# Four edits to the order of work in a tuned encoder layer: a PSUM copy moved to ScalarE, accumulating stores held back, a mixture put ahead, more places for split weights

## The chip, the cores and the metric

One core of a Trainium2 chip runs the whole kernel. The metric is the device time of one execution in microseconds (us), as the median of the runs shown. All matrix work is done in float32 accuracy by splitting each operand into a high and a low part, so one product is three matmuls: high by high, high by low, low by high.

## The reference, cut to what matters

The reference is one encoder layer with two branches side by side, applied to a prompt batch of 1024 rows and a sample batch of 512 rows with the same weights:

```python
h = rms_norm(x, pre_w)
cols = einsum('bsd,dc->bsc', h, w_in)              # one wide input projection
m_qk, m_v, m_o, m_z, m_i, m_f, a_qkv, a_z, gate = split(cols, ...)
y_m = mlstm_mixer(silu(conv(m_qk)), m_v, ...) * silu(m_z)      # branch A, both directions
y_a = dilated_attention(a_qkv, rel_table) * silu(a_z)          # branch B, three dilations
p_m = y_m @ w_pm
p_a = y_a @ w_pa
merged = sigmoid(gate_a) * p_m + sigmoid(gate_b) * p_a
y = x + rms_norm(merged @ w_out, post_w)
# the mixture inside dilated_attention, for 3 groups g:
w = exp(mx - max_g mx);  y_a = sum_g(w * o) / sum_g(w * den)
```

The outputs are y_prompt (1024 x 1024) and y_sample (512 x 1024).

## The kernel before, in words

The prompt batch is "the long set", the sample batch "the short set". The program runs in stages.

**First stage, up to some 965 us.** The input projection of the long set is done by the Strassen-Winograd scheme, two column units of 128 at a time, in `unit_pair` (from L827; 38 pairs). A pair is seven products m1, m6, m2, m7, m5, m4, m3 of 12 matmuls (128x512) each. The products lie in PSUM banks, the tile `d`. m2 is accumulated onto m1's bank and m3 onto m5's, so m3's first matmul can start only when m5 has been read out of that bank. `u2` and `u3` (in the profile the tile `pu`) are running sums in SBUF, `c` holds the four result blocks, `q[i][j]` are views of `c`. The weights come as `pw_raw` and `psum_w` and are split into high and low parts `phla` and `phlb` by ScalarE (L766 and L795 for the high part) and VectorE (L767 and L796 for the low part). After every pair the columns get what their kind asks for: convolution and tanh (`conv_unit`, L880 to L884), SiLU and others.

At the end of this stage the short set's input is turned (`turn_in`, L351 on TensorE, L357 on ScalarE, L358 on VectorE: the tiles `H`), and its own weights from `w_in` begin to be loaded into the two staging buffers `wraw` (L288) and split: the high part `wh` by ScalarE (L299), the low part `wl` (L305) by VectorE or, here, GpSimd.

**Middle.** The two branches of both sets, up to some 2028 us.

**Last stage, 2028 us to the end.** The short set's projections with `w_pm` (`proj_m`), `w_pa` (`proj_a`) and `w_out` (`final`) run on TensorE. Beside them stands what is left of other work:

- the 16 accumulating stores of y_prompt (L2494, 256 KB each; closures in the list `self.adds`, filled when the long set's output rows are done at L2493). A store adds to DRAM and is issued by GpSimd. `proj_m` pops one of them at every fourth step.
- GpSimd's queue, which also issues the loads of the pre-split weights (`wl<-pre`, `wh<-pre`, L832), of `w_pm` (`wraw<-w_pm`, L288), and of the mixture's inputs (`og_b` into V0a and V1a, `az_b`, `gt_b` into `gab`, all L276).
- the mixture of the short set, `combine`, four rounds of 128 rows. A round is `weigh` (a chain of small operations on `cw` and `wd`, L2086 to L2096), three `mix` (L2103), two `add` (L2109), then `turn` (L2114: four transposes `tp` on TensorE; L2116 on VectorE multiplies the result by `az`). Its result goes to DRAM (`ym_b`) by a store on SyncE's queue, and is loaded again from there as rows `ymr` and `sraw` (L276) to be split by ScalarE (L2209) and VectorE (L2210) for `proj_a`. I call the four turns turn 0 to turn 3; the last one is split straight from SBUF (L2120), without its 128 columns going through DRAM.

The order of each engine's instructions is fixed when the program is built: a scheduler places them by its own estimate of times and by priority. `high_priority()` lets an instruction go ahead of others that are ready, and `issue_after(x)` keeps an instruction behind x in its engine's order; it is no wait on the chip by itself. An engine runs its instructions in that order, so one that waits holds up those behind it.

Of the kernel before, what the change touches and what calls it, by code (L numbers as in the profile page):

```python
# [24 lines left out]
AF = mybir.ActivationFunctionType  # L25
# [181 lines left out]
class Net:  # L207
# [627 lines left out]
    def unit_pair(self, weights, H, sb, cp, ps):  # L835

        nc = self.nc
        wa, wb, (a11, a12), (s1, s2), s, places, (u2, u3) = weights
        split = self.pair_split

        def product(m, w, onto=None):
            p = onto or ps.tile([P, BLK], F32, name="d")
            for k in range(4):
                self.mm3(p, (w[0][:, k], w[1][:, k]), (H[0][m][:, k], H[1][m][:, k]), onto is None and k == 0, k == 3,
                         skip_group_check=onto is not None)
            return p

        nc.gpsimd.tensor_sub(s[:, 1], wa[:, 1], s[:, 1])
        s3, a22 = split(wb, places[0])
        c = [cp.tile([P, 2 + 2 * BLK], F32, name="c") for _ in range(2)]  # L850
        q = [[c[j][:, 1 + b * BLK:1 + (b + 1) * BLK] for b in range(2)] for j in range(2)]
        m1 = product(B11, a11)
        with self.tc.high_priority():
            nc.scalar.activation(u2, m1, AF.Copy)  # L854
        m6 = product(T2, s2)
        nc.vector.tensor_add(u2, u2, m6)
        m2 = product(B21, a12, m1)
        nc.scalar.activation(q[0][0], m2, AF.Copy)
        m7 = product(T3, s3)
        with self.tc.high_priority():  # L860
            nc.vector.tensor_sub(u3, u2, m7)
        m5 = product(T1, s1)
        with self.tc.high_priority():
            nc.vector.tensor_add(q[1][1], u3, m5)  # L864
        m4 = product(T4, a22)
        nc.vector.tensor_add(q[1][0], u3, m4)
        s4, = split(s[:, 1:2], places[1])
        m3 = product(B22, s4, m5)
        nc.vector.tensor_add(q[0][1], u2, m3)
        return c  # L870
# [1195 lines left out]
    def combine(self, T, bank, cs, ys, sb, azs, slow):  # L2066
# [3 lines left out]
        nc = self.nc  # L2070
# [76 lines left out]
        for t in range(T.n):  # L2147
# [7 lines left out]
            for i, step in enumerate(steps):  # L2155
                with ExitStack() as st:
                    if i < 6:
                        for x in (*self.splits, self.sum, *self.state, *self.keyed) if slow else (self.evicted, summed):
                            if x is not None:
                                st.enter_context(self.tc.issue_after(x.ins))  # L2160
                    last = step()
                    if i == 5:
                        summed = last
                if i == 6 and t == T.n - 1 and T in self.direct:
                    self.mixed.add(T)
                if slow:
                    yield
                elif i == 5:
                    for g in range(2) if t else ():
                        ahead(t + 1, g)  # L2170
                    yield
                    if t:
                        ahead(t + 1, 2)
                    yield
                elif i == 6:
                    ahead(t)
                    yield
# [382 lines left out]
    def branches(self, T, b, odd, before):  # L2560
# [3 lines left out]
        nc, a = self.nc, self.a  # L2564
# [8 lines left out]
        def proj_m(weights):  # L2573
# [3 lines left out]
            for ct in range(KT):  # L2577
                wm = weights()
                pm = self.dense()
                for k in range(KT):  # L2580
                    if k % 4 == 3 and self.adds:
                        self.adds.pop(0)()
                    c = slice(k * P, (k + 1) * P)
                    hi, lo = yb[k // 4]
                    self.mm3(pm, (wm[0][:, c], wm[1][:, c]), (hi[:, k % 4], lo[:, k % 4]), k == 0, k == KT - 1)
# [7 lines left out]
        def proj_a(weights):  # L2593
            for ct in range(KT):
                if ct % 2 == 0:
                    wa = weights()
                pa = self.dense()
                mh, ml = yb[ct // 4]
                yh, yl = ya[0]
# [447 lines left out]
```

## Time and profile before

| what | value |
|---|---|
| runs | 2189.52 us median of 3 (2189.27 to 2189.61) |
| profiled execution, its own time | 2190.96 us |
| profiled execution, span from the first to the last instruction | 2189.2 us, mean granted TensorE clock 0.997 |
| TensorE busy | 2161.0 us of the span (99%), 11530 matmuls |
| VectorE, ScalarE, GpSimd busy | 1503.4, 1106.3, 801.0 us (69%, 51%, 37%) |
| DMA | 469 MB, 214 GB/s on average |

The profiled execution is 1.44 us above the median of the runs. Its span leaves 1.8 us for what lies around the first and last instruction. The page gives for each group of instructions its busy time, the mean of one in ns and the idle time of its engine just before it with what ended it. A view of waits adds that idle time up by pairs of waiting and releasing lines; a timeline gives single rows: start, duration, engine, line, operation, tile, and in brackets the idle time before it with its releaser.

### The profile page before, as it was taken

The numbers are of one execution on the slowest core, as the hardware profiler recorded it, in microseconds if no ns is written. First come the engines' busy times: TensorE is split into PE (matmuls) and PEld (weight loads), VectorE is DVE, ScalarE is ACT, GpSimd is POOL, SyncE is SP. The second block draws the span as 40 slices with busy tenths as digits, with TensorE's granted clock in tenths as the row PEclk, the third lists the DMA queues.
The fourth block names the chain that finished last, engine by engine and source line by source line (L and its number), as shares of the span: only waits on it lengthen the run. The fifth ranks groups of instructions, "written<-read, shape, count | busy, mean of one in ns | idle before, by whom it ended". The sixth has DMA issues, their size and how long they took to land.

```text
span 2189.2 us, 33795 instructions
## 1 busy us (share of the span) xinstructions
PE 2161.0 (99%) x11530; PEld 1840.0 (84%) x11530; DVE 1503.4 (69%) x2923; ACT 1106.3 (51%) x2286; POOL 801.0 (37%) x1050
## 2 busy tenths in 40 slices
PE   9999999999999999999999999999999999999898
PEld 8988888888888888888888889999788888888686
DVE  8766575757788877537888766574667856675773
ACT  7322344454444444446777666665755544435422
POOL 1000444332333765325676660001035532331531
PEclk9999999999999999999999999999999999999999
DMA  5641687965456554358556558886767779886973
GB/s 215 191 141 65 210 271 245 301 218 182 177 190 217 198 188 175 135 192 270 176 184 228 164 159 263 254 244 179 224 237 239 266 254 330 287 275 208 265 239 114
DMA packets 234134, 469.04 MB, mean 214 GB/s; under 512 B 38281, under 2 KB 120393, under 8 KB 233834
## 3 DMA queue, kind: packets, MB, share of 16 engines
q1 hardware_dynamic: 199736, 343.81, 48.2%
q0 software_dynamic: 30624, 110.48, 15.7%
q10 hardware_dynamic: 3602, 12.59, 1.4%
q8 instruction: 91, 1.49, 0.3%
q14 instruction: 81, 0.66, 0.1%
HBM read 314.56 MB, written 156.43 MB: 215 GB/s over the span
## 4 chain that ended last, share of the span: by engine, by line
PE 90%; issue 3%; ACT 2%; DVE 2%; POOL 1%; DMA 1%; DVEq 0%; POOLq 0%; ACTq 0%
PE d L235 14%; PE d L237 13%; PE d L236 13%; PE dense L235 11%; PE dense L236 11%; PE dense L237 11%; PE lg L1851 2%; PE pt L1881 2%; PE o L1924 1%; PE num L235 1%; PE num L1544 1%; PE num L236 1%; PE num L237 1%; DMA wraw<-w_pm 1%; PE o L1903 1%
## 5 line engine op out<-in xcount | busy, mean ns | idle before, releaser
L235 PE MATMUL dense<-H,wh 128*128 128x512 f32 x712 | 288.6, 405 | 0.0
L237 PE MATMUL dense<-H,wl 128*128 128x512 f32 x712 | 279.0, 392 | 0.0
L236 PE MATMUL dense<-H,wh 128*128 128x512 f32 x664 | 260.4, 392 | 0.0
L235 PE MATMUL d<-Hh,phla 128*128 128x512 f32 x608 | 237.4, 390 | 0.4 <-ACT pu L854 0.3
L237 PE MATMUL d<-Hh,phla 128*128 128x512 f32 x608 | 236.6, 389 | 0.0
L236 PE MATMUL d<-Hl,phla 128*128 128x512 f32 x608 | 236.6, 389 | 0.0
L235 PE MATMUL d<-Hh,phlb 128*128 128x512 f32 x456 | 178.0, 390 | 3.6 <-DVE c L864 3.5
L237 PE MATMUL d<-Hh,phlb 128*128 128x512 f32 x456 | 177.5, 389 | 0.0
L236 PE MATMUL d<-Hl,phlb 128*128 128x512 f32 x456 | 177.4, 389 | 0.0
L237 PEld LDWEIGHTS dense<-H,wl 128*128 128x128 f32 x712 | 133.7, 188 | 29.9
L235 PEld LDWEIGHTS dense<-H,wh 128*128 128x128 f32 x712 | 134.3, 189 | 17.8 <-issue 0.9
L305 DVE TENSOR_TENSOR wl<-wraw,wh 128x1024 fp32r<-128x1024 f32 (+1 forms) x99 | 123.8, 1252 | 32.6 <-ACT wh L299 32.6
L785 POOL TENSOR_TENSOR psum_w<-pw_raw 128x512 f32<-128x512 f32 x38 | 52.4, 1380 | 245.0 <-DMA pw_raw<-w_in 144.1
L1870 DVE CUSTOM_DVE_ANT_0 ls<-lg,bias 128x256 f32<-128x256 f32 (+2 forms) x240 | 78.6, 350 | 90.8 <-PE lg L1851 67.3
L236 PEld LDWEIGHTS dense<-H,wh 128*128 128x128 f32 x664 | 125.3, 189 | 14.8 <-DVE H L2292 0.3
L235 PEld LDWEIGHTS d<-Hh,phla 128*128 128x128 f32 x608 | 114.1, 188 | 26.9 <-ACT pu L854 3.4
L237 PEld LDWEIGHTS d<-Hh,phla 128*128 128x128 f32 x608 | 114.1, 188 | 23.8
L236 PEld LDWEIGHTS d<-Hl,phla 128*128 128x128 f32 x608 | 114.2, 188 | 23.4
L299 ACT ACTIVATE wh<-wraw 128x1024 fp32r<-128x1024 f32 (+1 forms) x102 | 104.9, 1031 | 54.4 <-PE dense L236 39.1
L1874 ACT ACTIVATE ls<-ls,nm 128x256 f32<-128x256 f32 (+1 forms) x192 | 87.4, 456 | 76.2 <-DVE nm L1872 58.0
L235 PE MATMUL d<-v,Hh 128*128 128x484 f32 (+1 forms) x336 | 121.3, 361 | 0.1
L237 PE MATMUL d<-v,Hl 128*128 128x484 f32 (+1 forms) x336 | 120.6, 359 | 0.4 <-DVE Hl L475 0.4
(734 smaller groups left out, 5891.6 us busy)
## 6 DMA issues: line engine op xcount, KB each, us to landing
pw_raw<-w_in SPq DMA_DIRECT2D x76, 512.0 KB, 4.3
wraw<-w_in SPq DMA_DIRECT2D x63, 512.0 KB, 4.5
pw_raw<-w_q SPq DMA_DIRECT2D x44, 512.0 KB, 5.9
pre<-phlb SPq DMA_DIRECT2D x32, 512.0 KB, 4.3
aqk_a<-pwk SPq DMA_DIRECT2D x32, 512.0 KB, 7.0
pre<-phlb SPq DMA_DIRECT2D x16, 1024.0 KB, 7.7
wh<-pre POOLq DMA_DIRECT2D x27, 512.0 KB, 6.4
wl<-pre POOLq DMA_DIRECT2D x27, 512.0 KB, 6.5
```

The costliest lines, as they stand in the source:

```text
L235: nc.tensor.matmul(out, lh, rh, start=start, stop=False, **kw)
L236: nc.tensor.matmul(out, lh, rl, start=False, stop=False, **kw)
L237: nc.tensor.matmul(out, ll, rh, start=False, stop=stop, **kw)
L299: high = nc.scalar.activation(hi[:, :n], raw[:, :n], AF.Copy)
L305: low = (self.lows or nc.vector).tensor_sub(lo[:, :n], raw[:, :n], hi[:, :n].bitcast(F32))
L785: self.nc.gpsimd.tensor_add(s[:, 0], ws[1][:, 0], ws[1][:, 1])
L1544: nc.tensor.matmul(pn, hi[:, j], z[:, c1], start=j == 0 and z is v[0], stop=False)
L1851: nc.tensor.matmul(lg[:, hh], q[hh][:, qs], z.rearrange("p (n j) -> p n j", j=P)[:, pair], start=z is k[hh], stop=z is not k[hh])
L1870: nc.vector.tensor_tensor_reduce(out=ls[rows, hh], in0=ts["lg"][hh][rows, of], in1=bt[rows, hh, by], scale=1.0, scalar=NEG, op0=OP.add, op ...
L1874: self.held = self.held[-3:] + [nc.scalar.activation(ls[:, hh], ls[:, hh], AF.Exp, bias=nm[:, hh:hh + 1], accum_out=ot[:, 128 + hh:129 + hh])]
L1881: nc.tensor.transpose(pp[:, hh * nk + x], ts["ls"][:, hh, x * P:(x + 1) * P], self.ident)
L1903: nc.tensor.matmul(po[:, hh * 64:hh * 64 + 64], pt[:, hh * nk + x], vh(kt[x], hh), start=x == 0, stop=x == nk - 1)
```

## The change

Four places are edited.

1. `unit_pair`: m5 was read out of PSUM by VectorE (`q[1][1] = u3 + m5`, L864). Now ScalarE copies m5 to `q[1][1]`, and VectorE adds `u3` to it in SBUF. The subtraction that makes `u3` loses its high priority.
2. `combine`: the first six steps of a round (weigh, three mix, two add) of the short set are put under high priority.
3. `proj_m`: an accumulating store is kept behind the last weight load issued so far.
4. `proj_a`: from its third tile on, two more tiles (H0 and H3) serve as places for split weights, so those of `w_out` can be split earlier.

```diff
         m7 = product(T3, s3)
-        with self.tc.high_priority():
-            nc.vector.tensor_sub(u3, u2, m7)
+        nc.vector.tensor_sub(u3, u2, m7)
         m5 = product(T1, s1)
         with self.tc.high_priority():
-            nc.vector.tensor_add(q[1][1], u3, m5)
+            nc.scalar.activation(q[1][1], m5, AF.Copy)
+        nc.vector.tensor_add(q[1][1], q[1][1], u3)
...
+                    if i < 6 and not slow:
+                        st.enter_context(self.tc.high_priority())
                     last = step()
...
                     if k % 4 == 3 and self.adds:
-                        self.adds.pop(0)()
+                        with self.tc.issue_after(self.loaded.ins):
+                            self.adds.pop(0)()
...
                 if ct % 2 == 0:
                     wa = weights()
+                if ct == 2:
+                    self.more_places(weights.__self__, [[z[:, 1024 * i:1024 * (i + 1)] for i in range(2)] for z in map(self.take, ("H0", "H3"))])
                 pa = self.dense()
```

Line numbers after the edits shift by 2 to 5 (L2210 becomes L2212, L2494 becomes L2496, L2590 becomes L2593). The instructions are the same but for 38 more on ScalarE (the copies, L863 of the changed kernel). TensorE's and SyncE's order is unchanged. Where the order of the others moves:

**ScalarE, the end of the first stage.** `pu` is u2, `c<-d` at L858 is the copy of m2, `wh<-wraw` at L299 are the short set's first three `w_in` weights, `H<-d,prew` at L357 is the turned input. Before:

```order
L854 ACTIVATE pu_7217<-d 128x512
L858 ACTIVATE c<-d 128x512
L299 ACTIVATE wh_7347<-wraw_7345 128x1024
L299 ACTIVATE wh_7349<-wraw_7346 128x1024
L299 ACTIVATE wh_7351<-wraw_7345 128x1024
L357 ACTIVATE H_7383<-d,prew 128x512 x4
```

And now:

```order
L854 ACTIVATE pu_7254<-d 128x512
L858 ACTIVATE c<-d 128x512
L863 ACTIVATE c<-d 128x512
L299 ACTIVATE wh_7385<-wraw_7383 128x1024
L299 ACTIVATE wh_7387<-wraw_7384 128x1024
L299 ACTIVATE wh_7389<-wraw_7383 128x1024
L357 ACTIVATE H_7421<-d,prew 128x512 x4
```

The last pair's copy of m5 stands ahead of the three weight splits; m5 is the fifth of the pair's seven products, m2 the third.

**GpSimd, the beginning of the last stage**, the DMA issues (H, K are the rows to be added to y_prompt). Before:

```order
L2494 DMA y_prompt<-H_19572 128x512
L832 DMA wl_7350<-pre 128x1024
L832 DMA wh_7349<-pre 128x1024
L2494 DMA y_prompt<-K_20122 128x512
L832 DMA wl_7352<-pre 128x1024
L288 DMA wraw_7345<-w_pm 128x1024
L288 DMA wraw_7346<-w_pm 128x1024
L832 DMA wh_7351<-pre 128x1024
```

And now, from the same load of `wl` on:

```order
L832 DMA wl_7388<-pre 128x1024
L832 DMA wh_7387<-pre 128x1024
L832 DMA wl_7390<-pre 128x1024
L288 DMA wraw_7383<-w_pm 128x1024
L288 DMA wraw_7384<-w_pm 128x1024
L832 DMA wh_7389<-pre 128x1024
```

The stores have left this piece. They now begin behind the fifth `w_pm` load; around the load of V1a (the mixture's input of the fourth round) the order is now:

```order
L2496 DMA y_prompt<-H_19610 128x512
L2496 DMA y_prompt<-K_20160 128x512
L276 DMA az_20298<-az_b 128x4x128
L2496 DMA y_prompt<-H_19609 128x512
L2496 DMA y_prompt<-H_20046 128x512
L276 DMA V1a<-og_b 128x528 x3
L276 DMA gab<-gt_b 128x512 x2
L832 DMA sw<-pre 128x1024 x2
L2496 DMA y_prompt<-H_19609 128x512
L2496 DMA y_prompt<-H_20046 128x512
```

Ten of the sixteen stores stand ahead of V1a's loads of this round, all of them behind the fifth `w_pm` load; before, all sixteen stood ahead, twelve of them before that load.

**VectorE, the fourth round of the mixture and turn 3.** `cw` is the round's weights, `Q` its sum, `tp` the turned tile; `ymr` and `sraw` are the rows that come back from DRAM. Before:

```order
L2096 SCALAR_TENSOR_TENSOR cw_20628<-cw_20628,wd_20633 128x24
L2103 TENSOR_TENSOR Q_20265<-V1a,cw_20628 128x512 x3
L2109 TENSOR_TENSOR Q_20265<-Q_20265 128x512
L2590 SCALAR_TENSOR_TENSOR V1b<-gab,dense 128x512
L2109 TENSOR_TENSOR Q_20265<-Q_20265 128x512
L2210 TENSOR_TENSOR K_20462<-ymr_17685,H_20461 128x384
L2210 TENSOR_TENSOR K_20462<-sraw,H_20461 128x384
L2210 TENSOR_TENSOR K_20462<-ymr_17684,H_20461 128x384
L2116 TENSOR_TENSOR az_20260<-tp_20726,az_20260 128x512
```

And now:

```order
L2212 TENSOR_TENSOR K_20500<-ymr_17723,H_20499 128x384
L2096 SCALAR_TENSOR_TENSOR cw_20666<-cw_20666,wd_20671 128x24
L2212 TENSOR_TENSOR K_20500<-sraw,H_20499 128x384
L2103 TENSOR_TENSOR Q_20303<-V1a,cw_20666 128x512 x3
L2212 TENSOR_TENSOR K_20500<-ymr_17722,H_20499 128x384
L2109 TENSOR_TENSOR Q_20303<-Q_20303 128x512 x2
L2212 TENSOR_TENSOR K_20500<-ymr_17723,H_20499 128x384
L2116 TENSOR_TENSOR az_20298<-tp_20764,az_20298 128x512
```

Three splits of rows that come from DRAM now stand among the steps that turn 3 needs; before, they stood behind them.

**VectorE, the first round's end and turn 0.** `sw<-wraw` at L305 is a `w_pm` weight, `H<-H,ss,postw` at L2493 makes the rows of two later stores. Before:

```order
L2103 TENSOR_TENSOR X_20264<-V0a,cw_20410 128x512 x3
L305 TENSOR_TENSOR sw<-wraw_7345,sw 128x1024
L2109 TENSOR_TENSOR X_20264<-X_20264 128x512
L2493 SCALAR_TENSOR_TENSOR H_19571<-H_19571,ss,postw 128x512
L2493 SCALAR_TENSOR_TENSOR H_20008<-H_20008,ss,postw 128x512
L2109 TENSOR_TENSOR X_20264<-X_20264 128x512
```

And now:

```order
L2103 TENSOR_TENSOR X_20302<-V0a,cw_20448 128x512 x3
L2593 SCALAR_TENSOR_TENSOR V0b<-gab,dense 128x512
L305 TENSOR_TENSOR sw<-wraw_7383,sw 128x1024
L2109 TENSOR_TENSOR X_20302<-X_20302 128x512
L2495 SCALAR_TENSOR_TENSOR H_19609<-H_19609,ss,postw 128x512
L2495 SCALAR_TENSOR_TENSOR H_20046<-H_20046,ss,postw 128x512
L2495 SCALAR_TENSOR_TENSOR H_19609<-H_19609,ss,postw 128x512
L2109 TENSOR_TENSOR X_20302<-X_20302 128x512
```

The split of the weight still stands between the products and the sum, and three instead of two of the L2493 rows stand between the two additions; the eviction V0b, which stood ahead of the products, follows them.

## The prediction

> **What bounds the kernel now.** The page says that TensorE is busy for 2161.0 of 2189.2 us, so time can only come from its few waits. The first view is therefore that of TensorE's waits (waiting line, releasing line: us in total, times, longest):
>
> ```profile
> PE tp L2114 <- DVE cw L2086: 6.5, 2, 5.7
> PE d L235 <- DVE c L864: 3.5, 4, 0.9
> PE dense L235 <- DMA wh<-pre: 2.2, 1, 2.2
> PE dense L236 <- DVE wl L305: 0.8, 1, 0.8
> ```
>
> These four groups, 13.0 us, are what the four edits touch: the mixture's turns, m5's read-out, a weight load that lies behind the stores, and a late weight split of `w_out`. I then read the timelines around each.
>
> **Edit 1, the copy of m5.** One of the four stalls, on TensorE, ScalarE and VectorE:
>
> ```profile
> 517.57 0.39 PE L237 MATMUL d<-Hh,phlb 128*128 128x512 f32 x1
> 518.79 0.47 PE L235 MATMUL d<-Hh,phlb 128*128 128x512 f32 x1 [0.83 <-DVE c L864]
> ...
> 515.21 1.06 ACT L883 ACTIVATE pwk<-pwk 128x1024 f32<-128x1024 f32 x1 [2.94 <-DVE pwk L882]
> ...
> 517.97 0.67 DVE L864 TENSOR_TENSOR c<-pu,d 128x512 f32<-128x512 f32 x1
> ```
>
> m3 starts when L864 has ended. Its first matmul would come 0.23 us behind 517.57 and came at 518.79, and it took 0.47 instead of 0.39: 0.99 and 0.08 lost. Four such waits and a fifth too short for the view make some 4.4. The copy will stand on ScalarE behind L883, which ends at 516.27, and takes 0.6: it is through at 516.9, and TensorE wants the bank at 517.80. VectorE's add from SBUF then has nobody waiting. Gain **4.4**. The copy delays the split behind it on ScalarE by 0.6, to some 517.9; VectorE turned to that split only behind L864, at 518.6.
>
> But the same copy exists in the last pair, and there the order on ScalarE bites:
>
> ```profile
> 952.85 0.60 ACT L858 ACTIVATE c<-d 128x512 f32<-128x512 f32 x1 [4.84 <-PE d L237]
> 953.34 2.00 ACT L299 ACTIVATE wh<-wraw 128x1024 fp32r<-128x1024 f32 x2
> 960.22 1.06 ACT L299 ACTIVATE wh<-wraw 128x1024 fp32r<-128x1024 f32 x1 [4.88 <-DMA wraw<-w_in]
> 964.17 4.74 ACT L357 ACTIVATE H<-d,prew 128x512 fp32r<-128x512 f32 x8 [2.89 <-PE d L351]
> ...
> 956.89 2.68 SPq L288 DMA_DIRECT2D wraw<-w_in  x2
> ...
> 958.29 0.69 DVE L864 TENSOR_TENSOR c<-pu,d 128x512 f32<-128x512 f32 x1 [2.03 <-PE d L237]
> 964.89 3.38 DVE L358 SCALAR_TENSOR_TENSOR H<-d,prew,H 128x512 fp32r<-128x512 f32 x5 [0.34 <-ACT H L357]
> ...
> 965.61 1.58 PE L351 MATMUL d<-ident,xs 128*128 128x128 f32 x13
> ```
>
> The copy can run when m5 is done, at 958.29 (where L864 ran), so the first two L299 start at 958.8 instead of 953.34, 5.45 us later. Behind them, each 5.45 later: GpSimd's L305, the load of the third weight into the buffer that this frees (956.89 to 962.3; it took 3.2 to land, the third L299 starts on it at 960.22), so the third L299 runs from 965.7 to 966.7. L357 stands behind it: 966.6 instead of 964.17, and L358 2.45 later too. TensorE's transposes need their `d` tiles back: six groups of four fit, the seventh (966.15 by its place in the row of 13) needs the first L358, which ends at 965.6 before and at about 968.1 now. TensorE waits some 2.0 to 2.5 us there, and the next group a little. Loss **2.6**, between 0 (if more tiles were free) and 5.45.
>
> **Edit 3, stores held back.**
>
> ```profile
> 2038.54 0.54 POOL L832 DMA_DIRECT2D wh<-pre  x1 [2.23 <-issue]
> ...
> 2033.99 11.84 DMA wraw<-w_pm
> ...
> wh<-pre POOLq DMA_DIRECT2D x27, 512.0 KB, 6.4
> ```
>
> The first row is the late load, from the timeline, the second is the piece of the chain with the first `w_pm` loads, the third is the page's median from issue to landing. The late load was issued at 2038.54, 10.5 us ahead of TensorE's start at 2049.13. With the four stores out of the way it is issued some 4 us sooner, and at 6.4 us it lands near 2041: the wait of 2.24 goes, with 0.15 of slow start. Gain **2.4**. The `w_pm` loads land up to 11.84 - 6.4 = 5.4 us sooner.
>
> **Edit 2, turn 0.**
>
> ```profile
> 2070.36 1.23 DVE L305 TENSOR_TENSOR sw<-wraw,sw 128x1024 fp32r<-128x1024 f32 x1 [1.24 <-ACT sw L299]
> 2072.10 1.41 DVE L2493 SCALAR_TENSOR_TENSOR H<-H,ss,postw 128x512 f32<-128x512 f32 x2
> 2073.42 0.69 DVE L2109 TENSOR_TENSOR X<-X 128x512 f32<-128x512 f32 x1
> ...
> 2074.26 1.09 PE L2114 MATMUL tp<-ident,X 128*128 128x128 f32 x4 [5.67 <-DVE cw L2086]
> 2075.00 0.78 PE L235 MATMUL dense<-K,wh 128*128 128x512 f32 x1
> ...
> 2078.13 0.41 PE L236 MATMUL dense<-X,wh 128*128 128x512 f32 x1
> ...
> 2092.38 0.63 PE L2114 MATMUL tp<-ident,X 128*128 128x128 f32 x4 [0.82 <-DVE cw L2086]
> ...
> 2046.00:2052.00 6.00, 3.76 (x17) 2.81 (x17) 4.32 (x6) 4.10 (x8) 0.64 (x2) 1.00 1.08 309
> ```
>
> The last row is a stretch: length, busy time and count of TensorE, weight loads, VectorE, ScalarE and GpSimd, granted clock, DMA share, GB/s. The releaser's name hides it: the turn runs when the second L2109 has ended (2074.11). The wait cost more than itself. Behind it the transposes took 1.09 instead of 0.63, and seven matmuls took 3.13 us (2075.00 to 2078.13) instead of 7 x 0.23: some 1.9 us at a low clock. In all 5.67 + 1.9 + 0.15 of slow start = 7.7. What is left of it now: the wait for the weight (1.24) goes, two L2493 fewer and one eviction fewer stand ahead of the products (1.9), one L2493 and that eviction more between them and the turn (1.3), so 5.67 - 1.24 - 1.9 + 1.3 = 3.8; TensorE comes 2.4 sooner, and VectorE too by most of the 5.4 that the loads gain, I take 4.2: 2.0. So short a wait should not bring the low clock; the stretch with the wait of 2.24 has 1.00. Gain 7.7 - 2.0 = **5.7**, with 0.5 to 6.2 as bounds of what is left. Turn 2 (0.82) waited for a weight split that stood between its two additions and now follows them; gain **0.4**, from 0 to 1.0.
>
> **Edit 4.** The 0.76 us of the late `w_out` split and its slow start make 1.0; as work is pushed together ahead of it I count **0.6**.
>
> **What the edits make late: turn 3.** Here the new order costs. Before:
>
> ```profile
> 2093.76 0.36 SPq L251 DMA_DIRECT2D ym_b<-Q  x1
> 2096.10 0.33 SPq L276 DMA_DIRECT2D ymr<-ym_b  x1
> ...
> 2098.48 0.53 ACT L2209 ACTIVATE H<-ymr 128x384 fp32r<-128x384 f32 x1 [5.49 <-DMA ymr<-ym_b]
> 2099.21 0.53 ACT L2209 ACTIVATE H<-sraw 128x384 fp32r<-128x384 f32 x1 [0.20 <-DMA sraw<-ym_b]
> 2103.64 0.52 ACT L2209 ACTIVATE H<-ymr 128x384 fp32r<-128x384 f32 x1 [3.90 <-DMA ymr<-ym_b]
> ...
> 2104.20 0.56 DVE L2210 TENSOR_TENSOR K<-ymr,H 128x384 fp32r<-128x384 f32 x1 [3.87 <-ACT H L2209]
> ...
> 2100.45 0.60 PE L2114 MATMUL tp<-ident,Q 128*128 128x128 f32 x4
> ```
>
> VectorE's wait of 3.87 for the third row split hurt nobody, since turn 3 had its sum. Now that split stands ahead of both L2109. The third row still has to go out after turn 2 (store 2093.76, back from 2096.10) and come in (2103.64). On the clock of before, the split ends its slot at 2104.67, two L2109 take 1.4, turn 3 follows 0.15 later at 2106.2 where TensorE wants it at 2100.45: 5.75. If the third row came as close behind the second as the second behind the first (0.73), it would be 2.05. Above stands the queue: the stores moved out of the early stretch run here now.
>
> ```profile
> L251 SPq DMA_DIRECT2D ym_b<-X x1: 370/370/370, 2086.4 to 2086.4; - x1
> DMA to landing us min/median/max: 3.8/3.8/3.8
> ...
> 2058.00:2064.00 6.00, 6.00 (x27) 4.86 (x27) 5.13 (x13) 4.05 (x8) 4.68 (x8) 1.00 1.07 244
> ...
> L276 POOL DMA_DIRECT2D V1a<-og_b x3: 537/549/552, 2082.4 to 2083.5; - x3
> DMA to landing us min/median/max: 5.1/5.3/5.4
> ...
> 2092.15 0.16 DVE L2086 TENSOR_TENSOR cw<-V1a 128x8 f32<-128x8 f32 x1
> ```
>
> The first pair of rows is the store of turn 1, which went out in the saturated stretch and took 3.8 to land; that of turn 2 was back after 2.3, in an empty queue. I take the 3.8: 1.6 more. And of the four stores that stand beside V1a's loads in the new order, two will be under way while the rows come in: 0.26 MB at the 244 GB/s of the stretch with many stores is 1.07 us each, 2.1. So I take 5.75 + 1.6 + 2.1 = 9.45 us of waiting, nearer to the saturated row than to the empty one since the queue is fuller here now, and the low clock's 1.9 behind it as behind turn 0. Loss **11.35**, from 2.05 to some 16 (a wait of 14 and its 1.9).
>
> By the Trainium skill ("DMA: Bandwidth & Descriptors", Queues, rings and completion order) a DMA engine takes packets in turn from the queues that have work. By that rule GpSimd's stores never stand ahead of SyncE's transfers as a block, the store would take at most twice its 2.2 and the two stores would add nothing: 7.95 and 1.9, and the time would come out near 2188.5. The saturated store, 3.8 against 2.2, fits; for loads under stores no row stands.
>
> **The sum.** Gains 4.4 + 2.4 + 5.7 + 0.4 + 0.6 = 13.5; losses 2.6 + 11.35 = 13.95. The profiled execution, 2190.96, would become 2191.4; it stands 1.44 above the median of the runs, so on that scale 2189.52 + 0.45 = **2190.0**. The last stores and the last eviction do not move against the last matmul.
>
> **The rivals.**
> - Turn 3 waits little (faster). SyncE's transfers take turns with GpSimd's, so the third row comes 0.73 behind the second: 2.05 of waiting, no low clock, 13.5 - 2.6 - 2.05 = 8.85 gained: 2180.7. It counts as faster as long as wait and low clock together stay under 6.5, a wait of up to 4.6. For it: two of the three rows came fast (2098.48, 2099.21). Against: the third did not, in a queue without any store. The rule cited above speaks for this rival.
> - V1a is late (slower). The fourth round needs V1a; its loads now stand behind ten stores, all issued after the fifth `w_pm` load, where four stood before. Their landing at 2083.5 + 5.3 = 2088.8 may slip by six stores' 1.07, to 2095.2, less what the fifth load gains (up to 5.4). From there the round takes at most 8.3 (its first step at 2092.15, turn 3 at 2100.45), now with three row splits of 0.5 between: turn 3 at 2105.0 where TensorE, 8.5 ahead, wants it at 2091.95. That is 13.0 at worst by these rows, above the 9.45; with rows that also start late it decides from a wait of 13.4 on, where the sum is 4.4 slower. Price of a wait of 14: 2194.5.
> - The copy of m5 relieves nothing (slower): L883 ahead of it on ScalarE waited 2.94 us for VectorE in the row above, and where VectorE runs later the copy does too. Then 4.4 of gain is missing: 2194.4. Against it: in the row there is 0.9 us to spare.
>
> **How the numbers follow.** A change of 0.2%, 4.4 us, is about what a measurement of this kernel tells from none. Chances: the forecast, with turn 3's wait between 4.6 and 13.4, 0.45; little waiting at turn 3, 0.27; late V1a, 0.15; the copy without effect, 0.13. So faster 0.27, same 0.45, slower 0.28. The forecast's own range is 2185.1 to 2193.9. The whole range goes from 2181, the first rival's price, to 2197: a wait of 14 with its low clock, and turn 0 keeping 4 instead of 2, give 13.5 - 2.0 - 2.6 - 15.9 = 7.0 slower, 2196.5.
>
> **What the profile after would show.** Edit 1: no wait of `d` L235 for `c`, and L863 on ScalarE right behind L883; a wait of 2 to 2.5 us on L351 near 960 with ScalarE's third L299 ahead of it. Edit 3: no wait for `wh<-pre`, the first `w_pm` loads landing in about 6 us. Edit 2: some 2 us before turn 0 with the clock at 1.00; a long wait before turn 3 and matmuls at 0.43 us spacing behind it; VectorE's waits there named L2209 (rows) or V1a. The prediction is wrong if turn 3 has no wait above 4.6, if turn 0 still waits over 4, or if TensorE still waits for m5.

## The result and the profile after

The changed kernel takes 2202.61 us (2201.18 to 2203.76, 6 runs) against 2190.26 us (2189.27 to 2192.91, 6 runs) for the one before on the same chip: a ratio of 1.0054, 95% interval 1.0041 to 1.0067. It is 12.35 us slower. 2190.0 was forecast, with a range from 2181 to 2197; the time lies above it. The profiled execution took 2203.76 us (span 2202.0, mean granted clock 0.995), 12.8 us more than the profiled one of before.

First the view that the prediction began with, TensorE's waits, in the changed kernel (waiting line, releasing line: us in total, times, longest):

```profile
PE tp L2114 <- DVE Q L2109: 12.2, 1, 12.2
...
PE tp L2114 <- DVE cw L2086: 2.2, 2, 2.0
PE tp L2114 <- DVE X L2109: 2.1, 1, 2.1
PE d L351 <- DVE H L358: 1.8, 1, 1.8
PE d L235 <- ACT pu L854: 1.6, 1, 1.6
...
PE num L237 <- POOL scl L1291: 1.0, 1, 1.0
PE d L235 <- ACT c L863: 0.9, 3, 0.5
PE dense L235 <- ACT K L2614: 0.8, 1, 0.8
```

Set against the list of before: the waits for `wh<-pre` and for `wl` are gone, turn 0 (in the second row) went from 5.7 to 2.0, m5's bank from 3.5 in four waits to 0.9 in three. Against that stand 12.2 at turn 3, 2.1 at turn 2, and four waits that were not there before or, at L854, only 0.3 long (L351, L854, `scl`, `K`). `K` at L2614 is the high part of the merged product that is multiplied with `w_out`. The rows left out have little to do with the edits: at the start of the kernel 2.3 for `Hh` (3.2 before) and 1.1 for `u2b` (0.2 before), and 1.1 at L1773 in both.

A wait is not yet its cost, since a low clock can follow and since a later wait can swallow an earlier gain. So I laid the two profiled executions over each other, matmul by matmul in TensorE's order, and read how the distance between the starts changes at each place:

| place (time in the changed kernel) | predicted, us | measured, us |
|---|---|---|
| start of the kernel | none | -0.5 |
| m5's bank, first stage | -4.4 | -3.0 |
| L854, at 719.68 | none | +1.9 |
| border, L351, at 966.50 | +2.6 | +2.2 |
| `scl`, at 997 | none | +1.1 |
| middle, several small shifts | none | +0.5 |
| `wh<-pre` | -2.4 | -2.5 |
| turn 0, at 2070.27 | -5.7 | -5.5 |
| turn 1, at 2078.67 | none | +0.5 |
| turn 2, at 2088.27 | -0.4 | +2.8 |
| turn 3, at 2110.24 | +11.35 | +15.1 |
| L2614, at 2155.44 | none | +2.0 |
| late split of `w_out` | -0.6 | -1.4 |
| behind the last matmul | none | -0.4 |
| sum | +0.45 | +12.8 |

**Turn 3.** The timeline around it (start, duration, engine, line, tile; in brackets the idle time before and its releaser):

```profile
2089.89 0.36 SPq L251 DMA_DIRECT2D ym_b<-Q  x1
2097.10 0.33 SPq L276 DMA_DIRECT2D ymr<-ym_b  x1
...
2104.81 0.52 ACT L2211 ACTIVATE H<-ymr 128x384 fp32r<-128x384 f32 x1 [8.93 <-DMA ymr<-ym_b]
...
2094.47 0.17 DVE L2086 TENSOR_TENSOR cw<-V1a 128x8 f32<-128x8 f32 x1 [4.61 <-DMA V1a<-og_b]
...
2105.37 0.56 DVE L2212 TENSOR_TENSOR K<-ymr,H 128x384 fp32r<-128x384 f32 x1 [8.63 <-ACT H L2211]
2105.84 0.18 DVE L2096 SCALAR_TENSOR_TENSOR cw<-cw,wd 128x24 f32<-128x24 f32 x1
2106.41 1.89 DVE L2103 TENSOR_TENSOR Q<-V1a,cw 128x512 f32<-128x512 f32 x3
2108.68 1.41 DVE L2109 TENSOR_TENSOR Q<-Q 128x512 f32<-128x512 f32 x2
...
2110.24 1.08 PE L2114 MATMUL tp<-ident,Q 128*128 128x128 f32 x4 [12.19 <-DVE Q L2109]
...
2111.55 0.63 PE L236 MATMUL dense<-Q,wh 128*128 128x512 f32 x1
2111.97 0.63 PE L237 MATMUL dense<-K,wl 128*128 128x512 f32 x1
```

Read it from the bottom up. TensorE waits for the two L2109. They stand on VectorE behind a row split (L2212) that waited 8.63 us, and nothing behind it on VectorE ran in that time, though the fourth round needed no more than its last small step, three products and two additions. The split waited for ScalarE's high part, that for the rows' load, and the load was issued only at 2097.10, 7.2 us after the store of turn 2 (2089.89), and took 7.6 to land. Ahead of all that VectorE had already waited 4.61 for V1a. Behind the turn the matmuls come 0.43 us apart, against 0.23: the granted clock is at 0.50 until 2116.17, 5.9 us behind the start of the turn. At half speed that costs half of it, and the table has 2.95 us on top of the 12.19.

The queue that these transfers met, in stretches (length, busy time and count of TensorE, weight loads, VectorE, ScalarE, GpSimd, granted clock, DMA share, GB/s):

```profile
2058.00:2064.00 6.00, 6.00 (x27) 4.90 (x26) 5.83 (x16) 2.76 (x7) 1.89 (x3) 1.00 0.40 131
...
2090.00:2096.00 6.00, 6.00 (x23) 4.86 (x22) 1.19 (x5) 0.22 (x1) 2.08 (x5) 0.81 1.06 336
2096.00:2104.00 8.00, 2.04 (x10) 1.35 (x8) 0.64 (x4) 0.00 (x0) 1.47 (x2) 0.91 1.04 266
```

The first store is issued at 2063.45 (2029.97 before). In the 12 us before that the DMA share is 0.25 and 0.40; from 2070 to 2104 it is above 1, and TensorE does 2.04 us of work in the 8 us of the fourth row. Before, 2090 to 2096 had a share of 0.30. The stores left the stretch where the loads of `wh<-pre` and `w_pm` had stood among them, and now run in the one where the mixture's last round waits for its rows.

**Turn 2 and turn 0**, in the changed kernel's timeline of TensorE:

```profile
2070.27 0.63 PE L2114 MATMUL tp<-ident,X 128*128 128x128 f32 x4 [1.97 <-DVE cw L2086]
...
2071.20 0.39 PE L237 MATMUL dense<-K,wl 128*128 128x512 f32 x1
...
2088.27 0.63 PE L2114 MATMUL tp<-ident,X 128*128 128x128 f32 x4 [2.08 <-DVE X L2109]
...
2089.48 0.63 PE L237 MATMUL dense<-H,sw 128*128 128x512 f32 x1
```

Turn 0 came as predicted, wait 2.0 and no low clock (a matmul behind it takes 0.39, behind turn 2 it takes 0.63). At turn 2 the weight split between the additions is indeed gone, but VectorE now waits 1.55 us for an earlier weight and 0.37 for V0a inside the same round (0.15 and nothing before): both come by transfers, in stretches with a share above 1. How much of the wait that makes is not separated: it is 0.5 with smaller stores, but 0.4 with full ones where TensorE comes later to the turn (the first experiment). A wait of 2.08 is left, 1.3 more than before, and this one drew a low clock that the 1.97 at turn 0 did not; that makes the other 1.5 of the 2.8.

**First stage and border.** ScalarE and TensorE in the changed kernel:

```profile
515.64 1.06 ACT L883 ACTIVATE pwk<-pwk 128x1024 f32<-128x1024 f32 x1 [1.71 <-DVE pwk L882]
516.60 0.58 ACT L863 ACTIVATE c<-d 128x512 f32<-128x512 f32 x1
...
717.14 2.00 ACT L891 ACTIVATE pwk<-c 128x1024 f32<-128x1024 f32 x2 [2.94 <-DVE c L869]
719.05 0.58 ACT L854 ACTIVATE pu<-d 128x512 f32<-128x512 f32 x1
...
719.68 0.50 PE L235 MATMUL d<-Hh,phla 128*128 128x512 f32 x1 [1.57 <-ACT pu L854]
...
956.66 0.60 ACT L863 ACTIVATE c<-d 128x512 f32<-128x512 f32 x1 [4.84 <-PE d L237]
957.16 2.00 ACT L299 ACTIVATE wh<-wraw 128x1024 fp32r<-128x1024 f32 x2
964.02 1.06 ACT L299 ACTIVATE wh<-wraw 128x1024 fp32r<-128x1024 f32 x1 [4.87 <-DMA wraw<-w_in]
...
966.50 1.31 PE L351 MATMUL d<-ident,xs 128*128 128x128 f32 x8 [1.81 <-DVE H L358]
```

The copy stands right behind L883 and is through at 517.18, as the prediction had it. At 719 TensorE arrives 3.5 us earlier than before, but the chain that it needs there comes only 1.2 earlier (L854 at 719.05, before at 720.23): L854 reads m1 out, it stands behind L891, and L891 waited 2.94 us for VectorE. A part of the gain is paid back at the next thing that is late. At the border the order is the one predicted, the copy ahead of the two L299, the third L299 behind a load that came later by as much, L357 and L358 behind it. It also moved GpSimd's weight splits (L305 starts at 958.29, before at 954.47), which the prediction named and priced only through the load; `scl`, which TensorE waits for at 997, is GpSimd's work too. How the shift gets from one to the other is not shown: in between GpSimd also waits for loads.

### The profile page after: what moved, and what is told of

Same layout as the page of the kernel before. It is cut to its first block, busy times and chain, and to the rows that moved or that the text cites. A ratio compares the mean times of both kernels' runs of the same rounds, so it can differ in the third digit from the quotient of the medians.

```text
span 2202.0 us, 33824 instructions
## 1 busy us (share of the span) xinstructions
PE 2164.1 (98%) x11530; PEld 1840.2 (84%) x11530; DVE 1502.4 (68%) x2923; ACT 1122.2 (51%) x2324; POOL 808.2 (37%) x1050
## 4 chain that ended last, share of the span: by engine, by line
PE 81%; DVE 5%; DMA 5%; issue 4%; ACT 3%; POOL 1%; DVEq 0%; SPq 0%; POOLq 0%; ACTq 0%
PE d L235 11%; PE dense L235 11%; PE d L237 11%; PE d L236 11%; PE dense L236 11%; PE dense L237 11%; PE lg L1851 2%; PE pt L1881 1%; DVE pwk L882 1%; PE o L1924 1%; PE num L235 1%; PE num L237 1%; PE num L236 1%; PE num L1544 1%; DMA wraw<-w_out 1%
## 5 line engine op out<-in xcount | busy, mean ns | idle before, releaser
L305 DVE TENSOR_TENSOR wl<-wraw,wh 128x1024 fp32r<-128x1024 f32 (+1 forms) x96 | 120.0, 1252 | 30.2 <-ACT wh L299 30.1
L299 ACT ACTIVATE wh<-wraw 128x1024 fp32r<-128x1024 f32 (+1 forms) x99 | 101.7, 1031 | 45.2 <-PE dense L236 23.4
```

Of the source, the lines that this page charges most:

```text
L299: high = nc.scalar.activation(hi[:, :n], raw[:, :n], AF.Copy)
L305: low = (self.lows or nc.vector).tensor_sub(lo[:, :n], raw[:, :n], hi[:, :n].bitcast(F32))
```

## The experiments

Where an expectation uses letters: O is the theory that turn 3's wait comes from VectorE's order (row splits ahead of the last sum), P the rival that the high priority makes it, B the theory of the border. Times are medians, ratios are to the kernel before on the same chip. The experiments ran on three chips, on which the kernel before took 2189.93, 2190.73 and 2190.24 us, and the interval of a ratio is 2 to 4 us to either side; a difference of 1 us between two medians says little. HOLD stands for this edit, used in several of them:

```diff
                     if i == 5:
                         summed = last
+                        if not slow:
+                            self.last_sum = last
...
-                    nc.vector.tensor_sub(lo[:, z, :w], t[:, :w], hi[:, z, :w].bitcast(F32))
+                    with self.tc.issue_after(self.last_sum.ins) if row == 8 else ExitStack():
+                        nc.vector.tensor_sub(lo[:, z, :w], t[:, :w], hi[:, z, :w].bitcast(F32))
```

It keeps VectorE's splits of the mixture's rows (those from row 8 on) behind the second L2109 of the round; GpSimd's and SyncE's orders stay as they are, and on VectorE only the three row splits and one eviction change places with the sum.

### Rows behind the sum

The changed kernel with HOLD.

> The changed kernel, with one thing added: on VectorE the four row splits K<-ymr and K<-sraw are kept behind the second L2109 of the fourth round, so that turn 3 no longer stands behind them; GpSimd's and SyncE's queues stay as they are. Theory O (the order: turn 3's 12.2 us come from the three splits that stand ahead of its sum and wait for rows in a full queue): the wait shrinks to what V1a's landing leaves, about 2 to 3.5 us, and the low clock behind it goes: some 10.5 us faster than the changed kernel, 2191 to 2193.5. Rival Q (the late stores themselves: whoever stands first, V1a or the rows come late and TensorE waits for them, at turn 3 or in proj_a): less than 3 us faster, 2199.5 to 2202.5, with a wait of over 8 us in all behind turn 2.

2193.0 us, ratio 1.0013 [1.0004, 1.0023]: 9.6 us faster than the changed kernel. Turn 3 in its timeline:

```profile
2093.43 0.17 DVE L2086 TENSOR_TENSOR cw<-V1a 128x8 f32<-128x8 f32 x1 [4.69 <-DMA V1a<-og_b]
...
2097.78 1.41 DVE L2109 TENSOR_TENSOR Q<-Q 128x512 f32<-128x512 f32 x2
2102.81 0.56 DVE L2215 TENSOR_TENSOR K<-ymr,H 128x384 fp32r<-128x384 f32 x1 [3.62 <-ACT H L2213]
...
2099.34 1.09 PE L2114 MATMUL tp<-ident,Q 128*128 128x128 f32 x4 [4.00 <-DVE Q L2109]
```

VectorE still waits for the rows, 3.62 us (L2215 is L2212 of the changed kernel, its second half of the row splits), but now behind the sum, where nobody waits for it. V1a is as late as in the changed kernel (4.69 for 4.61). So the order makes 8.2 of turn 3's 12.2, and V1a with the chain behind it the 4.0 that stay, a little more than expected and with a low clock again. The row loads went out at 2098.1, 9.3 us after the store of turn 2: the queue did not get better, it only stopped mattering for the rows.

### Stores early

```diff
-                        with self.tc.issue_after(self.loaded.ins):
-                            self.adds.pop(0)()
+                        self.adds.pop(0)()
```

> The changed kernel without edit 3: the stores stand where they stood before, edits 1, 2 and 4 stay. On VectorE the row splits then stand behind the fourth round's sum again. Theory O: turn 3 has no wait above 1 us, the wait for wh<-pre (2.2) is back, edit 1 costs some 2: 2187 to 2193, depending on how much of turn 0's wait edit 2 alone takes away. Rival P (the high priority of the mixture makes turn 3 late): turn 3 still waits over 8 us, 2199 to 2203.

2191.38 us, 1.0009 [0.9999, 1.0018]. In its profiled execution, which at 2195.33 was the slowest of the ten, there is no wait at turn 3; the wait for `wh<-pre` is 3.4 with a low clock, turn 0 waits 3.7. Holding the stores is thus what makes the change slower, by some 11 us. In VectorE's order the row splits stand behind the sum here, and ahead of it where the stores are held, with the priority or without: edit 3 moved VectorE's instructions too, though it speaks of GpSimd's stores alone.

### No priority

```diff
-                    if i < 6 and not slow:
-                        st.enter_context(self.tc.high_priority())
```

> The changed kernel without edit 2: the mixture's steps lose their high priority, the stores stay held. On VectorE two row splits still stand ahead of the fourth round's first L2109 and the third between the two. Theory O: turn 3 still waits 10 to 14 us; the time stays within 3 us of the changed kernel, 2200 to 2206. Rival P: the wait falls under 5 us, 2190 to 2196.

2200.87 us, 1.005 [1.0033, 1.0067]. Turn 3 waits 9.9, turn 0 1.98. The priority is not the cause of turn 3's wait, and turn 0's gain, which the prediction put under edit 2, does not need edit 2.

### m5 on VectorE

Edit 1 undone, the rest as changed.

> The changed kernel without edit 1: VectorE reads m5 out of PSUM again. By the matmul-by-matmul comparison of the two profiles edit 1 won 3.0 us at m5's bank and lost 1.8 near 720, 2.1 near 966 and 1.35 near 997. Theory S (all four belong to edit 1): 2.2 us faster than the changed kernel, about 2200.4, with the four waits of 0.83 to 0.94 back and those near 720, 966 and 997 gone. Rival (the waits near 720 and 997 are chance of this run or of the later stage): 0 to 1 us faster or even slower, up to 2203.5.

2199.34 us, 1.0043 [1.0028, 1.0058]. The waits on L854, L351 and `scl` are gone, and m5's bank waits again:

```profile
PE d L235 <- DVE c L864: 4.9, 6, 1.1
```

By the starts of the matmuls (table above) the three losses that the expectation puts at 1.8, 2.1 and 1.35 are 1.9, 2.2 and 1.1. Edit 1, forecast to gain 1.8 net, costs 3.3 here by the medians. Its own places do not show that much. Laid over this kernel matmul by matmul, the changed one wins 4.5 us at m5's bank and loses 5.3 at L854, L351 and `scl`, 0.8 net. Most of the rest lies at turn 2, where the changed kernel has a low clock and this one, with a wait of 1.65, has none, and behind turn 3, where the low clock lasts 5.9 us in the changed kernel and 3.0 here. Whether edit 1 brings that or the place of the waits in this one execution (last section) is not shown.

### Small stores

```diff
-nc.gpsimd.dma_start(T.y[r0:r0 + P, c], y, accum_op=OP.add)
+nc.gpsimd.dma_start(T.y[r0:r0 + P, c.start:c.start + 64], y[:, :64], accum_op=OP.add)
```

> The changed kernel with each of the 16 accumulating stores cut to the first 64 of its 512 columns (the other columns of y_prompt stay x_prompt); the order of every engine is that of the changed kernel, only the bytes in the queue are fewer. Theory OQ (turn 3's 12.2 us are a product: the order makes turn 3 wait for the rows, and the stores in the queue make the rows late): turn 3's wait falls to 2 to 6 us, the store of Q lands in about 2 to 3 us instead of 7.1 and the rows in 2.4 to 5: 6 to 11 us faster than the changed kernel, 2192 to 2197. Rival O alone (the rows take that long in any queue): turn 3 keeps over 9 us, 2199 to 2203.

2193.34 us, 1.0011 [1.0002, 1.002], with the changed kernel's order on every engine. Turn 3 waits 7.3 us, more than expected; the row splits still stand in the way, here the first of them on VectorE:

```profile
2096.80 0.56 DVE L2212 TENSOR_TENSOR K<-ymr,H 128x384 fp32r<-128x384 f32 x1 [3.06 <-ACT H L2211]
```

The store of turn 2 landed in 3.1 us instead of 7.1, and VectorE waited 0.56 for V1a instead of 4.61. Order and queue both count, and the order costs some 5.6 us (7.3 less the 1.7 of the next one) even when the queue has room.

### Rows behind the sum, small stores

Both edits above together.

> Both reliefs at once: row splits behind the sum (as in e1) and each store cut to 64 of its 512 columns (as in e5; the other columns of y_prompt stay x_prompt). Theory OQ (order and full queue are the two causes, and nothing else): turn 3's wait falls under 1 us, from 12.2 in the changed kernel, 4.0 with the order alone mended and 7.3 with the queue alone relieved, and the low clock behind it goes: 2187 to 2190. Rival (a third cause at turn 3): 3 us or more of waiting stay there, 2191 or more.

2186.05 us, 0.9979 [0.997, 0.9989]. VectorE and TensorE at turn 3:

```profile
2088.52 0.16 DVE L2086 TENSOR_TENSOR cw<-V1a 128x8 f32<-128x8 f32 x1
...
2095.32 1.41 DVE L2109 TENSOR_TENSOR Q<-Q 128x512 f32<-128x512 f32 x2
2096.65 0.55 DVE L2215 TENSOR_TENSOR K<-ymr,H 128x384 fp32r<-128x384 f32 x1
...
2096.88 0.63 PE L2114 MATMUL tp<-ident,Q 128*128 128x128 f32 x4 [1.68 <-DVE Q L2109]
```

V1a is there when VectorE wants it, and no low clock follows. The wait is not under 1 as expected: another short piece of work stands in the way, an eviction of TensorE's own products (L2596 into V1b), which waits 2.48 us on VectorE ahead of the round's second step (argued from that row, no run took it away). That completes a square of turn 3's wait, with the times below it:

| | full stores | small stores |
|---|---|---|
| row splits ahead of the sum | 12.2 us (2202.61) | 7.3 us (2193.34) |
| row splits behind the sum | 4.0 us (2193.0) | 1.7 us (2186.05) |

Order and queue together make 10.5 of the 12.2.

### The last pair on VectorE

The changed kernel, with the last of the 38 pairs reading m5 out by VectorE as before (the subtraction that makes `u3` has its high priority back in that pair, too).

```diff
+        last = self.pairs_done == 38
...
+            if last:
+                nc.vector.tensor_add(q[1][1], u3, m5)
+            else:
+                nc.scalar.activation(q[1][1], m5, AF.Copy)
```

> The changed kernel, but in the last of the 38 pairs m5 is read out by VectorE as before; the other 37 copies stay. Theory B (the copy ahead of the three weight splits causes the wait near 966, and the later loads behind it the wait near 997): both go, 2.1 + 1.35 = 3.4 us faster, about 2199.2. Rival (the wait near 997 has another cause): only 2.1 faster, 2200.5, with the wait for scl still near 1 us.

2198.6 us, 1.0038 [1.0023, 1.0053]: 4.0 faster than the changed kernel, and the waits on L351 and on `scl` are both gone. So one copy out of 38 makes both. The two waits cost 3.5 when the two profiled executions are laid over each other, in line with the 3.4 expected.

### Edits 2, 3 and 4, rows behind the sum

No edit 1, with HOLD.

> Edits 2, 3 and 4 without edit 1, with the row splits kept behind the fourth round's sum. If edit 1's cost (3.3 us) and the order's (9.6 us) add up: 2193.0 - 3.3 = 2189.7, the time of before. Rival (the stage before sets other arrival times and the waits at the turns change): 2187 to 2193.

2189.81 us, 0.9996 [0.9987, 1.0006]. The forecast was 2189.7, and the costs of edit 1 and of the row splits add up by the medians; that they do to 0.1 is luck, given the chips and the intervals. As above, only 0.4 of edit 1's cost lies at its own places when this profile is laid over that of the rows behind the sum; 1.6 is a low clock behind turn 0 that follows a wait of 1.98 there and does not follow one of 1.95 here. What the held stores gain at turn 0 and `wh<-pre` they lose at turns 2 (1.8) and 3 (3.8).

### The first four stores held

As the last one, but only the first four stores are held.

```diff
+                        with self.tc.issue_after(self.loaded.ins) if len(self.adds) > 12 else ExitStack():
+                            self.adds.pop(0)()
```

> Edits 2 and 4 without edit 1; of edit 3 only the first four stores are held behind the loads, the other twelve are issued as they come; row splits behind the sum. Theory: the wait for wh<-pre (2.2) goes as with the whole edit 3, the queue is not left idle from 2050 to 2063, so V1a is in time for turn 3: no wait over 1 us there, 2184 to 2188, faster than before. Rival (four stores later push the w_pm loads and turn 0 waits 5 us or more again): 2188 to 2191.

2188.44 us, 0.999 [0.9981, 1.0], 0.4 above what was expected and inside the rival's range. The wait for `wh<-pre` is gone, turn 3 waits 0.3; but turn 0 keeps 4.9, as the rival had it. The gain at turn 0 came only where all stores were held behind the last load (2.0 above), and then the last round pays.

### The first four held, the copy in all pairs but the last

> The kernel of e8 (edits 2 and 4, the first four stores held, row splits behind the sum) with edit 1 in all pairs but the last. If edit 1 without its last pair is worth what e4 and e6 say (4.0 of loss gone against 3.3 of cost: 0.7 gained), 2187.7. Rival: nothing or a loss, since its gain is given back near 720: 2188.4 to 2190.

2185.93 us, 0.998 [0.997, 0.999], 4.3 us faster than before with the whole computation, and the lowest median of those that leave nothing out. It is 2.5 below the kernel without the copy, where 0.7 was expected; the two intervals overlap, and of the difference 1.3 lies in the first stage (3.1 won at m5's bank, 1.8 paid back at L854). Its waits at turns 0 and 1, and what VectorE waits for ahead of turn 0 (its L2121, L2116 and L2093 are L2114, L2109 and L2086 of the other kernels):

```profile
PE tp L2121 <- DVE cw L2093: 5.3, 2, 4.5
```

```profile
2067.96 1.23 DVE L305 TENSOR_TENSOR sw<-wraw,sw 128x1024 fp32r<-128x1024 f32 x1 [3.59 <-ACT sw L299]
```

What is left at turn 0 is a weight split that stands between the two additions and waits for its load.

### The first eight held

As the last one, with the first eight stores held (`> 8`).

> As e10, but the first eight stores are held instead of four. Theory: w_pm's loads run free until the fifth, as in the changed kernel, so turn 0 waits about 2 instead of 4.9, and with eight stores fewer to be done between turn 1 and turn 3 than in the changed kernel V1a is in time: 2183 to 2187. Rival: the stores meet V1a again and turn 3 waits 2 us or more: 2187 to 2191.

2197.99 us, 1.0035 [1.0022, 1.0048], and not the gain expected; turn 0 keeps 4.5. Turn 3 waits 13.4 us although HOLD is there. VectorE, then ScalarE:

```profile
2104.61 0.18 DVE L2098 TENSOR_TENSOR wd<-cw,V1a 128x24 f32<-128x24 f32 x1 [8.58 <-ACT cw L2096]
...
2102.58 0.52 ACT L2220 ACTIVATE H<-ymr 128x384 fp32r<-128x384 f32 x1 [12.42 <-DMA ymr<-ym_b]
...
2104.37 0.21 ACT L2096 ACTIVATE cw<-cw 128x24 f32<-128x24 f32 x1
```

It is the same trap on the next engine: the exponential of the mixture's weights, 0.21 us long, stands on ScalarE behind the row splits' high parts, which wait 12.42 us for the rows. HOLD named VectorE's half of the row split only.

### Held behind the load before the last

As the one with the copy in all pairs but the last, with every store held, but behind the weight load before the last one issued.

```diff
+            self.prior, self.loaded = getattr(self, "loaded", None), self.side.dma_start(raw[:, :kt * cols], src)
...
-                        with self.tc.issue_after(self.loaded.ins):
+                        with self.tc.issue_after(self.prior.ins):
```

> As e10, but every store is held behind the load before the last one instead of the last one, so the stores begin behind the fourth w_pm load, some 9 us sooner than in the changed kernel, while the queue was at a share of 0.25 to 0.40. Theory: the same work fits ahead of V1a and turn 0 waits 2 to 4, turn 3 under 1: 2183 to 2187. Rival: the third round's V0a, which now stands behind seven more stores, is late and turn 2 waits 3 us or more: 2187 to 2193.

2194.17 us, 1.0017 [1.0008, 1.0027]. VectorE ahead of turn 2:

```profile
2088.77 0.17 DVE L2093 TENSOR_TENSOR cw<-V0a 128x8 f32<-128x8 f32 x1 [6.59 <-DMA V0a<-og_b]
```

The stores met V0a's loads instead of V1a's, turn 2 waits 7.7 and turn 0 4.6. The rival in the expectation had the mechanism; the time is 1.2 above its range. Moving the stores by one load moved the collision by one round.

## Why the prediction was wrong

**Turn 3: the mechanism right, a row misread.** The row splits ahead of the sum, the late rows and the low clock are what the runs showed. The step that failed is the price of turn 2's store, "I take the 3.8: 1.6 more". The prediction takes 3.8 from a store "which went out in the saturated stretch", but the stretch shown beside it is 2058 to 2064, and that store, of turn 1, went out at 2086.44, when all sixteen accumulating stores had been issued and the DMA share was lower. Turn 0's store went out in a saturated stretch, and its row was in the trace of before (in the last two lines the number before the last is the DMA share):

```profile
L251 SPq DMA_DIRECT2D ym_b<-az x1: 371/371/371, 2076.1 to 2076.1; - x1
DMA to landing us min/median/max: 6.2/6.2/6.2
...
2076.00:2082.00 6.00, 6.00 (x23) 4.86 (x22) 4.52 (x12) 1.06 (x1) 2.18 (x4) 0.82 1.07 296
2082.00:2090.00 8.00, 8.00 (x38) 6.59 (x37) 7.37 (x18) 1.97 (x3) 2.60 (x5) 1.00 0.84 297
```

With 6.2 for 3.8 the same sum gives 5.75 + 4.0 + 2.1 = 11.85 of waiting. Measured are 12.19, with a store that took 7.1. The other term, the "two stores of 1.07", was too large: the third row took 7.7 us to come in, 6.7 before, so 1.0 more for 2.1. The low clock cost 2.95 for 1.9, since it lasted 5.9 us behind the long wait. Together that is 15.1 for 11.35. It stayed inside the bound of 16 that I gave it.

The rule of the Trainium skill ("DMA: Bandwidth & Descriptors", Queues, rings and completion order) that a DMA engine takes packets in turn from its queues was read there as "at most twice its 2.2". The runs show 7.1 under full stores, 3.1 with the stores cut to an eighth, and the 6.2 was there before. That reading, and the 2188.5 that came from it, did not hold in this queue.

**Turn 2: the step that failed is "gain 0.4, from 0 to 1.0".** I freed it of one weight split and did not ask when the round's other inputs would land now. Wait 2.08 and low clock: 3.2 us off, with a sign that my bounds left out.

**Edit 1: the working stopped at "VectorE's add from SBUF then has nobody waiting".** At the bank itself 3.0 of 4.4 came, and TensorE still waits there in three pairs (0.9). But TensorE that comes earlier meets the next late chain (L854, 1.9), which I had not looked for, and the last pair's copy makes `scl` late too (1.1). The border term itself was right, 2.2 for 2.6. At its own places edit 1 costs 2.2 in the table (0.8 against the kernel with m5 on VectorE, whose m5 waits are longer), where I forecast a gain of 1.8; the copy of the last pair alone makes 3.3 of loss.

**Right:** the `wh<-pre` term (2.5 for 2.4), turn 0 (5.5 for 5.7, with 1.97 of wait left where I wrote 2.0). But I put turn 0 under edit 2, and without edit 2 it is the same 1.98: it comes from the stores that are out of its way. The rival of a copy that relieves nothing fell with the row at 516.60. V1a, the other rival, was late in part: VectorE waited 4.61 for it, but the row splits ended last.

**The end:** the wait for the late split of `w_out` is gone, 1.4 for 0.6 gained. But 2.0 is lost at L2614, where I had nothing. TensorE's wait of 0.8 there stands in all kernels with sixteen full stores held behind the last load, with edit 1 or without, with edit 2 or without; it is gone with small stores, with early ones, and with four or eight held, and 0.2 where they are held behind the load before the last. So it comes with the held stores; by which way is not shown.

**The range.** Its upper end counted a longer wait at turn 3 and 2 us more at turn 0. The bounds that I gave the border and turn 2 did not enter, and the other places had none. Turn 3 and turn 0 stayed inside their bounds, so it is the other places that carried the time past the range. Of the 12.35 us missing, 3.8 are turn 3; turn 2 makes 3.2, L2614 2.0, L854 1.9, m5's bank 1.4 and `scl` 1.1, and the rest take 1.0 back.

## What to carry to other kernels

An engine runs its instructions in order, so for each wait that grows ask what short work on the critical chain is queued behind it, on every engine that takes part: holding one half of the row split moved the trap from VectorE to ScalarE. Before a row is taken as the price of a transfer under load, look up the DMA share where that very transfer went out. Transfers that are held back do not vanish, they meet whatever loads come next; holding four of the sixteen cleared one wait, eight or all of them starved a later round. And when a nearly full engine is made earlier in one place, look for the next chain that has not become earlier, and give the sum a bound for the places where you see nothing.

## What the hardware showed that was not expected

The low clock does not follow from the length of a wait alone. In the changed kernel 2.08 us at 2088.27 was followed by matmuls 0.43 apart and 1.97 us at 2070.27 was not; before, 2.24 at 2049.13 was not. What the drops have in common is where the wait lies. In the traces of all fourteen kernels the granted clock is either 1.00 or 0.50, and within one trace all its changes lie on a grid of 3.41 us. In the changed kernel (first number behind the length: TensorE busy; third from the end: granted clock):

```profile
2068.38:2071.80 3.42, 1.53 (x9) 1.39 (x10) 2.95 (x7) 0.05 (x1) 3.42 (x7) 1.00 0.89 180
2085.45:2088.86 3.41, 1.33 (x9) 0.88 (x8) 3.41 (x6) 1.06 (x1) 1.71 (x4) 1.00 1.12 248
2088.87:2092.27 3.40, 3.40 (x10) 2.65 (x9) 0.99 (x2) 0.00 (x0) 0.54 (x1) 0.50 1.09 275
```

TensorE was idle for 55% of the first window, around turn 0, and the clock stayed; it was idle for 61% of the second, around turn 2, and the clock was low in the next. In the fourteen traces, their first 30 us aside, every window that was idle for 58% or more was followed by a low one, and none that was idle for up to 57% was, with one exception: in the kernel with small stores the wait at the border, among short transposes, made 51% and was followed by a clock of 0.50.

```profile
967.43 1.46 PE L351 MATMUL d<-ident,xs 128*128 128x128 f32 x8 [1.74 <-DVE H L358]
```

The 2.24 of before fell into two windows, of which the fuller was idle for 49%. Once low, the clock stayed low behind windows that were idle for a quarter or more, and came back behind those idle for 15% or less. Against the start of the program the grid lies 0.4 to 3.3 us off, other in most traces, so a wait of about 2 us can go either way. By these shares a wait of 4 us always fills 58% of some window; that is worked out, and agrees with all longer waits here. The Trainium skill ("TensorE: Matmul & The Clock Gate", Part 1) says that the clock is set over a window of about 3.4 us that runs freely, which agrees with the grid. The table in that part of the Trainium skill has the low clock "after ≥1 idle window (~3.4µs)"; here windows idle for 58 to 61% were enough.

A store of 256 KB from SyncE took 2.2 us to land where the DMA share was 0.30 (before, 2090 to 2096), 3.8 at 0.84 and 6.2 at 1.07. In the changed kernel, at shares of 1.04 to 1.08, the three stores of the turns took 10.4, 9.7 and 7.1.
